# Instance normalisation over 3D volumes: the short steps run once for two tiles

## The chip, the cores and the metric

The kernel runs on one core of one Trainium2 chip. The metric is the device time of one execution in microseconds (us); smaller is better. A profiled execution of the kernel before gives the times of single instructions and of single transfers.

## The reference

```
x: (8, 64, 32, 64, 64) float32, eps = 1e-5
mean = np.mean(x, axis=(2, 3, 4), keepdims=True)
var  = np.var (x, axis=(2, 3, 4), keepdims=True)
out  = (x - mean) / np.sqrt(var + eps)
```

There are 8 x 64 = 512 instances (one for each batch and channel) of 131,072 numbers. Each instance is normalised with its own mean and variance. The input is 268.4 MB and so is the output; every number is read from memory (HBM) once and written once.

## The kernel before

**Tiles.** A tile is 8 instances, laid out as 128 partitions x 8192 floats (4 MB): an instance takes 16 partitions. There are 64 tiles. On-chip memory holds six of them, in `slot0` to `slot5`; tile k lives in slot k mod 6. The last tile is worked as two halves of 4 instances (128 x 4096), which lie side by side in slot 3.

**One tile's steps**, each done by one engine, with a semaphore from each to the next:

1. SP's queue loads the tile (L183 for the first six, L188 in the loop, L195 for the last ones).
2. VectorE (DVE) sums the left half of the columns (`reduce_sum`, L79), and ScalarE (ACT) sums the right half, by an Identity activation with an accumulator (L107). The results are two columns of a small tile.
3. TensorE multiplies the two columns by a block matrix `avg` that averages over the 16 partitions of an instance (L136, shown as two matmul passes). VectorE adds the two results and negates the sum: this is minus the mean (L82).
4. ScalarE squares the whole tile with minus the mean as its bias, and accumulates (L113). This is the longest instruction of the kernel.
5. TensorE averages the sums of squares (L143). ScalarE takes the root with eps added (L120), VectorE the reciprocal (L89) and the product with minus the mean, called the shift here (L92).
6. ScalarE normalises the left half of the columns in place (L123), VectorE the right half (L95).
7. ScalarE's queue issues the store of the tile (L130) when both are done. SP waits for this store before it loads the next tile into the same slot.

Every engine takes the tiles strictly in order, in program order: ten rounds of a loop over the six slots (60 tiles), then three single tiles and the two halves. Nothing of tile k+1 is started on ScalarE before the store of tile k is issued. On SP, the loads wait in slot order for `stored[s]`. There is one set of semaphores, one small tile and one PSUM tile for each slot (`LANES` = 8, with the two halves).

ScalarE loads a table of functions (`ACT_TABLE_LOAD`) ahead of the first L107 and the first L120 of each loop round, 20 times in all. The five engines' programs stand in an `nc.Block()`, at whose end all engines meet; ScalarE waits there for all stores first.

Of the kernel before, what the change touches and what calls it, by code (L numbers as in the profile page):

```python
# [9 lines left out]
def kernel(  # L10
# [6 lines left out]
    nc = tc.nc  # L17
    fp32 = mybir.dt.float32
    Alu = mybir.AluOpType
    Act = mybir.ActivationFunctionType  # L20

    P = 128
# [4 lines left out]

    COLS = 8192
    SLOTS = 6
    FULL = P * COLS // n_elem  # L30
    n_tiles = n_inst // FULL
    ROUNDS = (n_tiles - 1) // SLOTS
    LANES = SLOTS + 2

    x_f = x.rearrange("b c d h w -> (b c) (d h w)")
    out_f = out.rearrange("b c d h w -> (b c) (d h w)")
    x_t = x_f.rearrange("(k i) (s f) -> k (i s) f", i=FULL, s=P // FULL)
    out_t = out_f.rearrange("(k i) (s f) -> k (i s) f", i=FULL, s=P // FULL)
    x_h = x_f.rearrange("(k i) (s f) -> k (i s) f", i=FULL // 2, s=2 * P // FULL)
    out_h = out_f.rearrange("(k i) (s f) -> k (i s) f", i=FULL // 2, s=2 * P // FULL)  # L40

    ctx.enter_context(tc.tile_critical(name="norm"))  # L42

    def sbuf(name, shape, dtype=fp32):
        return ctx.enter_context(nc.sbuf_tensor(name, shape, dtype))

    slots = [sbuf(f"slot{s}", [P, COLS]) for s in range(SLOTS)]

    unused = sbuf("unused", [P, COLS], mybir.dt.uint8)
    eps_t = sbuf("eps_t", [P, 1])  # L50
    avg = {n: sbuf(f"avg{n}", [P, P]) for n in (FULL, FULL // 2)}
    small = [sbuf(f"small{i}", [P, 8]) for i in range(LANES)]
    psum = [
        ctx.enter_context(nc.psum_tensor(f"psum{i}", [P, 512], fp32))
        for i in range(LANES)
# [2 lines left out]
    def semaphores(name, n):  # L58
        return [ctx.enter_context(nc.semaphore(f"{name}{i}")) for i in range(n)]

    ready = semaphores("ready", 1)[0]
    landed = semaphores("landed", LANES)
    summed = semaphores("summed", LANES)
    meaned = semaphores("meaned", LANES)
    centred = semaphores("centred", LANES)
# [2 lines left out]
    rooted = semaphores("rooted", LANES)  # L68
    scaled = semaphores("scaled", LANES)
    shifted = semaphores("shifted", LANES)  # L70
    done = semaphores("done", LANES)
    stored = semaphores("stored", LANES)

    def on_vector(eng, t, lane, n, c1, c2, c16):
        w = t.shape[1] // 2
        a = small[lane]
        eng.reduce_sum(  # L79
            out=a[:, 0:1], in_=t[:, :w], axis=mybir.AxisListType.X  # L80
        )._wait_ge(landed[lane], c16).then_inc(summed[lane], 1)
        eng.tensor_reduce(  # L82
            out=a[:, 2:3],
            in_=psum[lane][:, 0:2],
            axis=mybir.AxisListType.X,
            op=Alu.add,
            negate=True,
        )._wait_ge(meaned[lane], c1).then_inc(centred[lane], 1)
        eng.reciprocal(out=a[:, 5:6], in_=a[:, 4:5])._wait_ge(  # L89
            rooted[lane], c1  # L90
        ).then_inc(scaled[lane], 1)
        eng.tensor_mul(out=a[:, 6:7], in0=a[:, 2:3], in1=a[:, 5:6])._wait_ge(  # L92
            scaled[lane], c1
        ).then_inc(shifted[lane], 1)
        eng.tensor_scalar(  # L95
            out=t[:, w:],
            in0=t[:, w:],
            scalar1=a[:, 5:6],
            scalar2=a[:, 6:7],
            op0=Alu.mult,  # L100
            op1=Alu.add,
        )._wait_ge(shifted[lane], c1).then_inc(done[lane], 1)

    def on_scalar(eng, t, lane, n, c1, c2, c16, dst):
        w = t.shape[1] // 2
        a = small[lane]
        eng.activation(  # L107
            out=unused[:, w : 2 * w],
            in_=t[:, w:],
            func=Act.Identity,  # L110
            accum_out=a[:, 1:2],
        )._wait_ge(landed[lane], c16).then_inc(summed[lane], 1)
        eng.activation(  # L113
            out=unused[:, : 2 * w],
            in_=t,
            func=Act.Square,
            bias=a[:, 2:3],
            accum_out=a[:, 3:4],
        )._wait_ge(centred[lane], c1).then_inc(squared[lane], 1)
        eng.activation(  # L120
            out=a[:, 4:5], in_=psum[lane][:, 2:3], func=Act.Sqrt, bias=eps_t[:, 0:1]
        )._wait_ge(varied[lane], c1).then_inc(rooted[lane], 1)
        eng.activation(  # L123
            out=t[:, :w],
            in_=t[:, :w],
            func=Act.Identity,
            scale=a[:, 5:6],
            bias=a[:, 6:7],
        )._wait_ge(shifted[lane], c1).then_inc(done[lane], 1)
        eng.dma_start(out=dst, in_=t)._wait_ge(done[lane], c2).then_inc(  # L130
            stored[lane], 16
        )

    def on_tensor(eng, t, lane, n, c1, c2, c16):
        a = small[lane]
        eng.matmul(  # L136
            out=psum[lane][:, 0:2],
            lhsT=avg[n][:],
            rhs=a[:, 0:2],
            start=True,  # L140
            stop=True,
        )._wait_ge(summed[lane], c2).then_inc(meaned[lane], 1)
        eng.matmul(  # L143
            out=psum[lane][:, 2:3],
            lhsT=avg[n][:],
            rhs=a[:, 3:4],
            start=True,
            stop=True,
        )._wait_ge(squared[lane], c1).then_inc(varied[lane], 1)


    rest = [
        (x_t[k], out_t[k], slots[k % SLOTS][:], k % SLOTS, k // SLOTS + 1, FULL)
        for k in range(ROUNDS * SLOTS, n_tiles - 1)
    ]
    last = (n_tiles - 1) % SLOTS
    for h in range(2):
        k = 2 * (n_tiles - 1) + h
        half = slots[last][:, h * COLS // 2 : (h + 1) * COLS // 2]
        rest.append((x_h[k], out_h[k], half, SLOTS + h, 1, FULL // 2))  # L160

    def over_tiles(eng, step, with_target=False):
        counts = [
            ctx.enter_context(eng.register(f"{step.__name__}_c{m}")) for m in (1, 2, 16)
        ]
        for c, m in zip(counts, (1, 2, 16)):
            eng.reg_mov(c, m)
        with eng.Fori(0, ROUNDS) as it:
            for s in range(SLOTS):
                more = (out_t[it * SLOTS + s],) if with_target else ()  # L170
                step(eng, slots[s][:], s, FULL, *counts, *more)
            for c, m in zip(counts, (1, 2, 16)):
                eng.reg_add(c, c, m)
        for _, dst, t, lane, c, n in rest:
            more = (dst,) if with_target else ()
            step(eng, t, lane, n, c, 2 * c, 16 * c, *more)

    block = ctx.enter_context(nc.Block())

    @block.sync  # L180
    def _(eng):
        for s in range(SLOTS):
            eng.dma_start(out=slots[s][:], in_=x_t[s]).then_inc(landed[s], 16)  # L183
        c16 = ctx.enter_context(eng.register("load_c16"))
        eng.reg_mov(c16, 16)
        with eng.Fori(1, ROUNDS) as it:
            for s in range(SLOTS):
                eng.dma_start(out=slots[s][:], in_=x_t[it * SLOTS + s])._wait_ge(  # L188
                    stored[s], c16
                ).then_inc(landed[s], 16)  # L190
            eng.reg_add(c16, c16, 16)
        for src, _, t, lane, c, n in rest:
            behind = lane if lane < SLOTS else last
            uses = c - 1 if lane < SLOTS else ROUNDS
            eng.dma_start(out=t, in_=src)._wait_ge(stored[behind], 16 * uses).then_inc(  # L195
                landed[lane], 16
            )

    @block.gpsimd
    def _(eng):  # L200
        count = 0
        for n, m in avg.items():
            split = P // n

            eng.memset(m[:], 1.0 / n_elem).then_inc(ready, 1)  # L205
            count += 1
            for sign in (-1, 1):
                eng.affine_select(  # L208
                    out=m[:],
                    in_=m[:],  # L210
                    pattern=[[sign * split, n], [0, split]],
                    compare_op=Alu.is_ge,
                    fill=0.0,
                    base=0 if sign < 0 else split - 1,
                    channel_multiplier=-sign,
                )._wait_ge(ready, count).then_inc(ready, 1)
                count += 1
        eng.memset(eps_t[:], eps_f).then_inc(ready, 1)  # L218

    READY = 3 * len(avg) + 1  # L220

    @block.vector
    def _(eng):
        over_tiles(eng, on_vector)

    @block.tensor
    def _(eng):
        eng.wait_ge(ready, READY)
        over_tiles(eng, on_tensor)

    @block.scalar
    def _(eng):
        eng.wait_ge(ready, READY)
        over_tiles(eng, on_scalar, with_target=True)

        for s in range(SLOTS):
            uses = ROUNDS + sum(1 for r in rest if r[3] == s)
            eng.wait_ge(stored[s], 16 * uses)
        for s in range(SLOTS, LANES):
            eng.wait_ge(stored[s], 16)  # L240


# [33 lines left out]
```

## Time and profile before

| | |
|---|---|
| four timed runs | 1248.35 to 1248.66 us, median 1248.54 us |
| the profiled execution | 1248.72 us, of which the profile's span is 1247.0 us |
| moved by the DMA queues | 536.90 MB, half in, half out |
| ScalarE (ACT) busy | 986.0 us, 79% of the span |
| VectorE (DVE) busy | 467.9 us, 38% |
| TensorE (PE) busy | 76.3 us, 6% |
| first load issued, first store issued | 1.03 us, 31.87 us |
| last store issued | 1234.04 us |

All times inside the profile are counted from the start of the span. "ACTq" and "SPq" are the instruction queues of ScalarE and SyncE, which issue stores and loads. Of the DMA queues, q1 carries the loads and q10 the stores; both are served by the same 16 DMA engines. A DMA share of 1.00 in a stretch means that these 16 were busy all the time; in short stretches the share and the rate also move a little with the transfers that lie across the edges.

### The profile page before, as it was taken

Reading aid. Unit: us, or ns where it says so; the run is one execution under the profiler, and the core shown is the slowest. Engines: PE = TensorE matmul, PEld = TensorE weight load, DVE = VectorE, ACT = ScalarE, POOL = GpSimd, SP = SyncE. Lnnn points to the kernel's source line nnn. Section 1 sums busy time; section 2 is a strip of 40 time slices with the busy share of each in tenths; the row PEclk is TensorE's granted clock in tenths of the full one; section 3 lists DMA queues with packets and bytes.
Section 4 is the critical chain, followed back from the end, with each engine's and each line's share of the span. In section 5 each row is a group of like instructions: output and inputs, shape, how many; then the busy total and the mean of one; then the engine's idle time right before and its main releaser. Section 6 shows DMA issues by size and latency. Waiting matters only on the chain.

```text
span 1247.0 us, 1819 instructions
## 1 busy us (share of the span) xinstructions
PE 76.3 (6%) x260; PEld 65.2 (5%) x260; DVE 467.9 (38%) x325; ACT 986.0 (79%) x410; POOL 1.9 (0%) x11
## 2 busy tenths in 40 slices
PE   0000000000000000000000000000000000000000
PEld 0000000000000000000000000000000000000000
DVE  2344334433334334343343433433334333343331
ACT  5888888887787878778777878787787878778774
POOL 0000000000000000000000000000000000000000
DMA  9999999999999999999999999999999999999998
GB/s 403 420 436 434 426 437 435 434 427 436 434 435 429 434 435 435 431 430 436 435 432 429 436 435 433 428 437 435 434 427 436 435 434 429 434 435 435 430 431 373
DMA packets 18722, 536.90 MB, mean 431 GB/s; under 512 B 2080, under 2 KB 2080, under 8 KB 2080
## 3 DMA queue, kind: packets, MB, share of 16 engines
q1 hardware_dynamic: 9360, 268.44, 50.0%
q10 hardware_dynamic: 9360, 268.44, 49.9%
q14 instruction: 2, 0.02, 0.0%
HBM read 268.44 MB, written 268.44 MB: 431 GB/s over the span
## 4 chain that ended last, share of the span: by engine, by line
ACT 48%; DVE 29%; another core or an unknown queue 13%; PE 6%; issue 1%; DMA 1%; ACTq 0%; DVEq 0%; SPq 0%
ACT unused L113 37%; DVE small L79 18%; DVE slot L95 8%; ACT slot L123 4%; ACT unused L107 4%; PE psum L136 3%; PE psum L143 3%; ACT small L120 1%; ACT L120 1%; DMA slot<-in_x_dram 1%; DVE small L89 1%; DVE small L82 1%; DVE small L92 1%; ACTq L130 0%
## 5 line engine op out<-in xcount | busy, mean ns | idle before, releaser
L113 ACT ACTIVATE unused<-slot,small 128x8192 uint8<-128x8192 f32 (+1 forms) x65 | 456.1, 7016 | 90.2 <-DVE small L82 90.2
L79 DVE TENSOR_REDUCE small<-slot 128x1 f32<-128x4096 f32 (+1 forms) x65 | 282.9, 4353 | 163.7 <-DMA slot<-in_x_dram 163.7
L107 ACT ACTIVATE unused<-slot 128x4096 uint8<-128x4096 f32 (+1 forms) x65 | 231.7, 3564 | 82.2 <-DMA slot<-in_x_dram 77.1
L123 ACT ACTIVATE slot<-slot,small 128x4096 f32<-128x4096 f32 (+1 forms) x65 | 243.6, 3748 | 27.6 <-DVE small L92 27.6
L89 DVE RECIPROCAL small<-small 128x1 f32<-128x1 f32 x65 | 10.7, 164 | 533.8 <-ACT small L120 533.8
L95 DVE TENSOR_SCALAR slot<-slot,small 128x4096 f32<-128x4096 f32 (+1 forms) x65 | 154.6, 2379 | 2.4
L136 PE MATMUL psum<-small,avg 128*128 128x2 f32 x130 | 38.2, 363 | 674.3 <-DVE small L79 548.8
L136 PEld LDWEIGHTS psum<-small,avg 128*128 128x128 f32 x130 | 32.6, 311 | 679.7 <-DVE small L79 553.1
L143 PE MATMUL psum<-small,avg 128*128 128x1 f32 x130 | 38.2, 363 | 480.6 <-ACT unused L113 480.6
L143 PEld LDWEIGHTS psum<-small,avg 128*128 128x128 f32 x130 | 32.6, 312 | 486.2 <-ACT unused L113 486.2
L120 ACT ACTIVATE small<-psum,eps_t 128x1 f32<-128x1 f32 x65 | 17.0, 261 | 37.4 <-PE psum L143 37.3
L82 DVE TENSOR_REDUCE small<-psum 128x1 f32<-128x2 f32 x65 | 10.3, 159 | 63.2 <-PE psum L136 63.2
L107 ACT ACT_TABLE_LOAD x10 | 12.8, 1283 | 10.4 <-ACT slot L123 7.1
L120 ACT ACT_TABLE_LOAD x10 | 12.8, 1283 | 0.2
L113 ACT ACTIVATION_READ_ACCUMULATOR unused<-slot,small 128x1 f32 x65 | 12.1, 186 | 0.0
L107 ACT ACTIVATION_READ_ACCUMULATOR unused<-slot 128x1 f32 x65 | 12.1, 186 | 0.0
L92 DVE TENSOR_TENSOR small<-small 128x1 f32<-128x1 f32 x65 | 10.3, 159 | 2.2
L208 POOL TENSOR_SCALAR_AFFINE_SELECT avg<-avg 128x128 f32<-128x128 f32 x4 | 1.3, 324 | 0.3
L205 POOL MEMSET avg<- 128x128 f32 x2 | 0.4, 204 | 0.5 <-SPq L42 0.5
L257 POOL MEMSET const-bfloat16-1.0<- 128x1 bf16 x1 | 0.1, 101 | 0.0
L257 POOL MEMSET const-uint8-127<- 128x1 uint8 x1 | 0.1, 101 | 0.0
L218 POOL MEMSET eps_t<- 128x1 f32 x1 | 0.1, 99 | 0.0
(2 smaller groups left out, 0.2 us busy)
## 6 DMA issues: line engine op xcount, KB each, us to landing
slot<-in_x_dram SPq DMA_DIRECT2D x63, 4096.0 KB, 52.6
out_dram<-slot ACTq DMA_DIRECT2D x63, 4096.0 KB, 45.4
slot<-in_x_dram SPq DMA_DIRECT2D x2, 2048.0 KB, 55.6
out_dram<-slot ACTq DMA_DIRECT2D x2, 2048.0 KB, 14.7
```

What stands on the lines that cost most here:

```text
L79: eng.reduce_sum(out=a[:, 0:1], in_=t[:, :w], axis=mybir.AxisListType.X)._wait_ge(landed[lane], c16).then_inc(summed[lane], 1)
L82: eng.tensor_reduce(out=a[:, 2:3], in_=psum[lane][:, 0:2], axis=mybir.AxisListType.X, op=Alu.add, negate=True,)._wait_ge(meaned[lane], c1) ...
L89: eng.reciprocal(out=a[:, 5:6], in_=a[:, 4:5])._wait_ge(rooted[lane], c1).then_inc(scaled[lane], 1)
L92: eng.tensor_mul(out=a[:, 6:7], in0=a[:, 2:3], in1=a[:, 5:6])._wait_ge(scaled[lane], c1).then_inc(shifted[lane], 1)
L95: eng.tensor_scalar(out=t[:, w:], in0=t[:, w:], scalar1=a[:, 5:6], scalar2=a[:, 6:7], op0=Alu.mult, op1=Alu.add,)._wait_ge(shifted[lane], ...
L107: eng.activation(out=unused[:, w : 2 * w], in_=t[:, w:], func=Act.Identity, accum_out=a[:, 1:2],)._wait_ge(landed[lane], c16).then_inc(sum ...
L113: eng.activation(out=unused[:, : 2 * w], in_=t, func=Act.Square, bias=a[:, 2:3], accum_out=a[:, 3:4],)._wait_ge(centred[lane], c1).then_in ...
L120: eng.activation(out=a[:, 4:5], in_=psum[lane][:, 2:3], func=Act.Sqrt, bias=eps_t[:, 0:1])._wait_ge(varied[lane], c1).then_inc(rooted[lane ...
L123: eng.activation(out=t[:, :w], in_=t[:, :w], func=Act.Identity, scale=a[:, 5:6], bias=a[:, 6:7],)._wait_ge(shifted[lane], c1).then_inc(don ...
L136: eng.matmul(out=psum[lane][:, 0:2], lhsT=avg[n][:], rhs=a[:, 0:2], start=True, stop=True,)._wait_ge(summed[lane], c2).then_inc(meaned[lan ...
L143: eng.matmul(out=psum[lane][:, 2:3], lhsT=avg[n][:], rhs=a[:, 3:4], start=True, stop=True,)._wait_ge(squared[lane], c1).then_inc(varied[la ...
L208: eng.affine_select(out=m[:], in_=m[:], pattern=[[sign * split, n], [0, split]], compare_op=Alu.is_ge, fill=0.0, base=0 if sign < 0 else s ...
```

## The change

Six slots are worked as three pairs. In the loop, both tiles of a pair go through each step together: the two sums, one averaging matmul over four columns, one negated addition, two squares, one averaging matmul over two columns, one root, one reciprocal, one product, then normalise and store the first tile, normalise and store the second. The rest (three single tiles, two halves) is worked one by one as before, with semaphores and small tiles of their own. `landed`, `stored` and `done` stay one for each tile; the other semaphores are one for each pair. The second square of a pair waits for the first. The table with the root is loaded once, at the start, by `preload_act_table`. The `nc.Block()` is gone: each engine's program is written straight into its queue, and SP, not ScalarE, waits for the stores at the end.

The core of the diff (`on_tensor` and the loop are changed in the same manner):

```
-    def on_vector(eng, t, lane, n, c1, c2, c16):
+    def on_vector(eng, tiles, marks, lane, n, c):
+        k = len(tiles)
...
+        for j, (t, m) in enumerate(zip(tiles, marks)):
+            eng.reduce_sum(
+                out=a[:, 2 * j : 2 * j + 1], in_=t[:, :w], axis=mybir.AxisListType.X
+            )._wait_ge(landed[m], c[16]).then_inc(summed[lane], 1)
         eng.tensor_reduce(
-            out=a[:, 2:3],
-            in_=psum[lane][:, 0:2],
+            out=a[:, 4 : 4 + k],
+            in_=psum[lane][:, 0 : 2 * k].rearrange("p (k h) -> p k h", h=2),
...
-        eng.reciprocal(out=a[:, 5:6], in_=a[:, 4:5])._wait_ge(
-            rooted[lane], c1
+        eng.reciprocal(out=a[:, 10 : 10 + k], in_=a[:, 8 : 8 + k])._wait_ge(
+            rooted[lane], c[1]
         ).then_inc(scaled[lane], 1)
...
+        for j, (t, m) in enumerate(zip(tiles, marks)):
+            eng.tensor_scalar(
+                out=t[:, w:],
...
+            )._wait_ge(shifted[lane], c[1]).then_inc(done[m], 1)
+    def on_scalar(eng, tiles, marks, lane, n, c, targets):
...
+        for j, (t, m) in enumerate(zip(tiles, marks)):
+            eng.activation(
+                out=unused[:, j * w : (j + 1) * w],
+                in_=t[:, w:],
+                func=Act.Identity,
+                accum_out=a[:, 2 * j + 1 : 2 * j + 2],
+            )._wait_ge(landed[m], c[16]).then_inc(summed[lane], 1)
+        for j, t in enumerate(tiles):
+            eng.activation(
+                out=unused[:, : 2 * w],
+                in_=t,
+                func=Act.Square,
+                bias=a[:, 4 + j : 5 + j],
+                accum_out=a[:, 6 + j : 7 + j],
+            )._wait_ge(*((squared[lane], c["odd"]) if j else (centred[lane], c[1]))).then_inc(
+                squared[lane], 1
+            )
         eng.activation(
+            out=a[:, 8 : 8 + k],
+            in_=psum[lane][:, 4 : 4 + k],
+            func=Act.Sqrt,
+            bias=eps_t[:, 0:1],
+        )._wait_ge(varied[lane], c[1]).then_inc(rooted[lane], 1)
+        for j, (t, m) in enumerate(zip(tiles, marks)):
+            eng.activation(
+                out=t[:, :w],
+                in_=t[:, :w],
+                func=Act.Identity,
+                scale=a[:, 10 + j : 11 + j],
+                bias=a[:, 12 + j : 13 + j],
+            )._wait_ge(shifted[lane], c[1]).then_inc(done[m], 1)
+            eng.dma_start(out=targets[j], in_=t)._wait_ge(done[m], c[2]).then_inc(
+                stored[m], 16
+            )
...
         with eng.Fori(0, ROUNDS) as it:
-            for s in range(SLOTS):
-                more = (out_t[it * SLOTS + s],) if with_target else ()
-                step(eng, slots[s][:], s, FULL, *counts, *more)
...
+            for g in range(GROUPS):
+                of = [g * SHARED + j for j in range(SHARED)]
+                more = ([out_t[it * SLOTS + s] for s in of],) if with_target else ()
+                step(eng, [slots[s][:] for s in of], of, g, FULL, c, *more)
...
-    block = ctx.enter_context(nc.Block())
...
+    nc.scalar.preload_act_table(Act.Sqrt)
+    nc.scalar.wait_ge(ready, set_by)
+    over_tiles(nc.scalar, on_scalar, with_target=True)
```

The order of the loads on SP, their sizes and the semaphores that they wait for are the same as before.

## The prediction

> **What bounds the kernel now.** I read the page first: the busy shares, the forty slices and the DMA queues.
>
> ```profile
> span 1247.0 us, 1819 instructions
> ...
> PE 76.3 (6%) x260; PEld 65.2 (5%) x260; DVE 467.9 (38%) x325; ACT 986.0 (79%) x410; POOL 1.9 (0%) x11
> ...
> ACT  5888888887787878778777878787787878778774
> ...
> DMA  9999999999999999999999999999999999999998
> GB/s 403 420 436 434 426 437 435 434 427 436 434 435 429 434 435 435 431 430 436 435 432 429 436 435 433 428 437 435 434 427 436 435 434 429 434 435 435 430 431 373
> ...
> q1 hardware_dynamic: 9360, 268.44, 50.0%
> q10 hardware_dynamic: 9360, 268.44, 49.9%
> ```
>
> ScalarE is the busiest engine, but no slice of it is full. The DMA row is full in every slice but the last, and the two queues together took 99.9% of the 16 engines' time. The chain of waits names ScalarE's square (37%), but a chain only follows one path back. So I asked for the stretches, to see what the DMA engines do from stage to stage:
>
> ```profile
> 5.00:30.00 25.00, 1.18 (x4) 1.00 (x4) 6.86 (x5) 14.43 (x7) 0.00 (x0) 1.00 1.02 439
> 34.00:38.00 4.00, 0.59 (x2) 0.50 (x2) 0.94 (x2) 3.13 (x3) 0.00 (x0) 1.00 1.04 385
> 200.00:1200.00 1000.00, 61.07 (x208) 52.17 (x208) 380.21 (x260) 795.59 (x329) 0.00 (x0) 1.00 1.00 433
> 1224.00:1243.00 19.00, 1.18 (x4) 1.00 (x4) 3.70 (x5) 7.75 (x6) 0.00 (x0) 1.00 0.97 417
> ```
>
> The last two columns are the DMA share and the rate. Loads alone (the first row), loads with stores (the third) and stores alone (the last) run at nearly the same rate, with a share of about 1. So the bound is the time of the 16 engines: 4.194 MB / 433 GB/s = 9.69 us for a tile one way, 128 x 9.69 = 1240 us in all. What is left of the span is 2.0 us before the first byte and about 4 us from 1243 on, in which the last engines and the closing barriers finish.
>
> The waits say the same: ScalarE waits for loads, and SP for stores, which are the DMA engines again.
>
> ```profile
> ACT unused L107 <- DMA slot<-in_x_dram: 77.1, 44, 8.9
> ...
> SPq L188 <- DMA out_dram<-slot: 1049.3, 54, 52.4
> ```
>
> **The change, part by part.** The time can only move if the DMA engines stand idle where they did not, or at the two ends.
>
> *The short steps.* The groups by line:
>
> ```profile
> L107 ACT ACT_TABLE_LOAD x10 | 12.8, 1283 | 10.4 <-ACT slot L123 7.1
> L120 ACT ACT_TABLE_LOAD x10 | 12.8, 1283 | 0.2
> ...
> L92 DVE TENSOR_TENSOR small<-small 128x1 f32<-128x1 f32 x65 | 10.3, 159 | 2.2
> ```
>
> L82, L89, L92 and L120 run 35 times instead of 65 (30 pairs and five singles). That is 30 x (159 + 164 + 159 + 261) ns = 22 us of DVE and ACT time. Of the 20 table loads one is left: 19 x 1.283 = 24.4 us of ACT. All of it is hidden by the DMA engines: 0 us. It would be worth up to 46 us if ScalarE set the pace, which it does not while it has 77 us of waiting for loads.
>
> The Trainium skill (ScalarE: Activation LUTs, "What ACT_TABLE_LOAD costs") puts a switch at about 1283 ns and 1380 ns more for a drain; the row agrees on the first, and the 0.2 us of idle time ahead of L120's loads shows no drain here. By that page the 19 would be an estimated 50 us, equally hidden.
>
> *The pair's chain.* This part could hurt: no store of a pair is issued before both tiles are squared. These rows fix the start:
>
> ```profile
> 13.53 3.62 ACT L107 ACTIVATE unused<-slot 128x4096 uint8<-128x4096 f32 x1 [8.94 <-DMA slot<-in_x_dram]
> ...
> 18.83 7.12 ACT L113 ACTIVATE unused<-slot,small 128x8192 uint8<-128x8192 f32 x1 [1.59 <-DVE small L82]
> ...
> 31.87 0.40 ACTq L130 DMA_DIRECT2D out_dram<-slot  x1
> ...
> 49.30 0.34 ACTq L130 DMA_DIRECT2D out_dram<-slot  x1
> ```
>
> Tile 0 lands at 13.5, tile 1 one tile later at 23.2. From landing to square takes 18.83 - 13.53 = 5.3, so the squares start at 28.5. Two squares with their accumulator reads take 2 x 7.31 + 0.06 = 14.7 (to 43.2); matmul, root, reciprocal and shift about 1.35 (0.68 of them between square and root, 0.68 to L123, as in the second tile); each normalise 3.80 and each store issue about 0.4. Store 0 is issued at 48.4 instead of 31.87, store 1 at 52.6. In steady work a pair costs ScalarE 2 x 3.85 + 0.86 + 14.7 + 1.35 + 2 x 4.2 = 33.0 us. The DMA engines need 2 x 19.4 = 38.8 for it. Before, the spacing of stores at full ScalarE pace is 49.30 - 31.87 = 17.4, against 19.4. So ScalarE's load falls from 90% to 85%, and it is late only at the start.
>
> *Is there always something to transfer at the start?* Before, the first store's bytes began some 4.2 us after its issue (the disturbance at 34 to 38 us), and its slot's load was issued 24.8 us after it (31.87 to 56.69). Now store 0 joins at 48.4 + 4.2 = 52.6. By then loads alone have moved about (52.6 - 2.8) / 9.69 = 5.1 of six tiles, so 8.4 us of work are left. The two queues share the engines evenly, so the loads run dry after 16.7 us, at 69.3. Store 0 is complete at about 72, the next load is issued then and joins at 73 to 76. Meanwhile store 1 runs alone; at 76 it has about half its work left and ends near 85. Store 2 is issued at 52.6 + 0.4 + 7.7 + 0.86 + 14.7 + 1.35 + 3.8 = 81.4 and joins at 85.6; load 6 then has about 5 us of work left. So about 5 us of queued transfers is the thinnest point, and no gap opens. Afterwards each pair gains 38.8 - 33.0 = 5.8 us and the queues fill. Cost: 0 us; if the chain were x us longer than 5 us, x.
>
> *A queue that starts anew.* At 34 to 38 us the stores' queue starts beside the running loads, and the rate is 385 instead of 433 GB/s: (433 - 385) / 433 x 4 = 0.44 us lost. That happens today as well. New is that the loads' queue runs dry once, at 69 to 76 us. No row shows such a restart; bounds are 0 and, with a second one near 85 us, 2 x 0.44 = 0.9. I take one, 0.44 us.
>
> The Trainium skill (DMA: Bandwidth & Descriptors, "Anatomy of one DMA — SWDGE (gpsimd) path") speaks against letting queues run dry: it gives each transfer about 2.0 us of fixed cost, for GpSimd's path. A restart at that price would make an estimated 1.6 us more than mine; no run here shows it on these queues.
>
> *The block.* Dropping it takes one meeting of all engines from the end. ScalarE's last wait for a store (L240) passes at 1245.5; the block's barrier rows lie at 1245.6 to 1245.9, and other barriers follow until 1247.0. I take -0.4 us; bounds are 0 and -1.5 (all after 1245.5).
>
> *The tail* is one by one as before. The last half landed at 1223.59 and its store was issued at 1234.04, while stores ran without a break until 1243. Pairing holds stores back, so at the end loads are further ahead and more stores are left to cover this chain: 0 us.
>
> Sum, against the profiled execution: 1248.72 + 0.44 - 0.4 = 1248.8; the median of the runs lies 0.2 below the profiled one: 1248.5 us.
>
> **Rivals.** *A: slower, the loads' queue runs dry at every tile.* A load is issued when a store has landed. If the next one always joins just after the last has ended, the queue restarts 58 times instead of once: 58 x 0.44 = 25 us, 1274 us. For: at the first turn it does run dry. Against: by my schedule load 7 is issued at about 86 while load 6 runs until about 96, and load 8 at about 105 while load 7 runs until 115; some 10 us of lead against 4.2 us to join. It decides where the lead falls below 4.2 us. A start that is several us thinner than I count (a gap of up to 5 us) lies between it and my forecast.
>
> *B: ScalarE sets the pace before and the savings show.* Then up to 46 us come off: about 1202. Against: a DMA share of 1.00 over 1000 us, at one rate in every mix. For: only the chain.
> The Trainium skill (DMA: Bandwidth & Descriptors, "Where 436 GB/s comes from") names 435 GB/s as the engines' ceiling and about 358 as the memory's share of a core; the 433 measured refutes the second here and sits at the first, so a faster rate is not to be had.
>
> *C: the change does not do what it says,* because a table load returns with every root in the loop. Then 30 or more loads of 1.283 us come back, 1.3 to 2.6 us a pair, within the 5.8 us of room: still 1248.5 in steady work, up to 1 us more at the start. It ends with the forecast.
>
> **How the numbers follow.** About 0.2% (2.5 us) is what a measurement of this kernel can tell from no change. My forecast (with C) gets 0.82, rival A and a gap at the start 0.14, B and anything else that gains over 2.5 us 0.04. The forecast's bounds give 1248.5 - 1.5 to 1248.5 + 0.9; I stretch the upper end to 1252 for part of a gap at the start, and leave out A's 1274 and B's 1202. Range 1247.0 to 1252.0.
>
> **What would show it.** Right: DMA share 1.00 and 433 GB/s over 200 to 1200 us; first stores at 48 and 52 us; one ACT_TABLE_LOAD; ScalarE busy about 986 - 24.4 - 30 x 0.26 = 954 us, and more waiting for loads than 77 us; loads resuming near 72 us; the last store issued before 1234 us. Wrong: a rate below 430 GB/s in the middle, a share below 1 at 70 to 110 us, or a span that ends more than 2.5 us from 1247.

## The result, and the profile after

| | before | after |
|---|---|---|
| median of the runs beside each other | 1248.52 us (62 runs) | 1249.87 us (42 runs) |
| ratio | | 1.002, 95% interval 1.0012 to 1.0028 |
| the profiled execution | 1248.72 us, span 1247.0 | 1248.59 us, span 1246.4 |

The change makes the kernel slower by 0.2%, a little more than its measurement is uncertain; the forecast had been "the same", 1248.5 us. Two of the 42 runs (1270.5 and 1271.8 us) are over 1.5% above the fastest, count as slow and are left out of the ratio. Over all the runs of the changed kernel, 71 with the profiled ones and the repeats told below, there are three groups: 6 cheap runs at 1248.6 to 1249.0 us (the profiled one is among them), 51 common ones at 1249.2 to 1250.5, and 14 long ones at 1252.9 to 1271.8. Of 168 runs of the kernel before one is above 1252 us (1253.3). So there are two questions: what costs the common run 1.3 us, and what makes one run in five long. Both are in the ratio.

The page of the changed kernel, in the rows that were shown of the kernel before:

```profile
span 1246.4 us, 1451 instructions
...
PE 41.1 (3%) x140; PEld 35.1 (3%) x140; DVE 448.6 (36%) x235; ACT 953.4 (76%) x361; POOL 1.9 (0%) x11
...
DMA  9999999999999999999999999999999999999998
GB/s 404 420 426 434 437 435 426 434 437 435 426 434 437 434 427 434 437 434 427 434 437 434 427 434 436 435 427 434 436 435 427 433 437 435 427 433 437 429 433 385
```

ScalarE's 986.0 us became 953.4, as worked out (954), and the DMA row did not notice. The stretches of the same execution:

```profile
34.00:38.00 4.00, 0.00 (x0) 0.00 (x0) 0.00 (x0) 3.97 (x3) 0.00 (x0) 1.00 1.04 451
200.00:1200.00 1000.00, 32.33 (x110) 27.56 (x110) 359.27 (x184) 774.36 (x288) 0.00 (x0) 1.00 1.00 433
1224.00:1243.00 19.00, 0.00 (x0) 0.00 (x0) 0.55 (x1) 1.29 (x1) 0.00 (x0) 1.00 0.98 421
```

433 GB/s and a share of 1.00 over 1000 us, exactly as before. The groups and the waits of ScalarE:

```profile
L252 ACT ACT_TABLE_LOAD x1 | 1.3, 1283 | 1.0 <-SPq L44 1.0
```

```profile
ACT unused L134 <- DMA slot<-in_x_dram: 149.8, 27, 10.9
```

One table load is left, and what ScalarE saved it spends waiting for loads: 149.8 us instead of 77.1. The order of time at the start:

```profile
28.20 7.12 ACT L141 ACTIVATE unused<-slot,small 128x8192 uint8<-128x8192 f32 x1 [1.58 <-DVE small L106]
...
35.45 7.12 ACT L141 ACTIVATE unused<-slot,small 128x8192 uint8<-128x8192 f32 x1
...
47.86 0.40 ACTq L164 DMA_DIRECT2D out_dram<-slot  x1
52.13 0.35 ACTq L164 DMA_DIRECT2D out_dram<-slot  x1
...
72.43 16.28 SPq L212 DMA_DIRECT2D slot<-in_x_dram  x2
...
80.36 0.34 ACTq L164 DMA_DIRECT2D out_dram<-slot  x1
```

Stores at 47.9, 52.1 and 80.4 us (forecast 48.4, 52.6, 81.4), the first load into a used slot at 72.4 (forecast 72). So the schedule was right to about a microsecond. But this is one of the six cheap executions: it contains neither the 1.3 us nor a long run.

### The profile page after: what moved, and what is told of

Its sections match the earlier page's. It is cut to its first block, busy times and chain, and to the rows that moved or that the text cites. A ratio compares the mean times of both kernels' runs of the same rounds, so it can differ in the third digit from the quotient of the medians.

```text
span 1246.4 us, 1451 instructions
## 1 busy us (share of the span) xinstructions
PE 41.1 (3%) x140; PEld 35.1 (3%) x140; DVE 448.6 (36%) x235; ACT 953.4 (76%) x361; POOL 1.9 (0%) x11
## 4 chain that ended last, share of the span: by engine, by line
DMA 54%; ACT 25%; another core or an unknown queue 12%; DVE 4%; PE 2%; issue 1%; ACTq 0%; SPq 0%
DMA out_dram<-slot 33%; DMA slot<-in_x_dram 21%; ACT unused L141 16%; ACT slot L157 6%; DVE small L103 4%; ACT unused L134 2%; PE psum L171 1%; PE psum L178 1%; ACT small L150 0%; ACTq L164 0%; SPq L212 0%; DVE small L113 0%; DVE small L106 0%; DVE small L116 0%
## 5 line engine op out<-in xcount | busy, mean ns | idle before, releaser
L134 ACT ACTIVATE unused<-slot 128x4096 uint8<-128x4096 f32 (+1 forms) x65 | 231.6, 3563 | 169.2 <-DMA slot<-in_x_dram 149.8
L113 DVE RECIPROCAL small<-small 128x2 f32<-128x2 f32 (+1 forms) x35 | 5.8, 165 | 498.2 <-ACT small L150 498.2
L120 DVE TENSOR_SCALAR slot<-slot,small 128x4096 f32<-128x4096 f32 (+1 forms) x65 | 152.0, 2376 | 1.3
L171 PE MATMUL psum<-small,avg 128*128 128x4 f32 (+1 forms) x70 | 20.6, 365 | 708.3 <-DVE small L103 614.9
L171 PEld LDWEIGHTS psum<-small,avg 128*128 128x128 f32 x70 | 17.6, 312 | 711.2 <-DVE small L103 617.2
L178 PE MATMUL psum<-small,avg 128*128 128x2 f32 (+1 forms) x70 | 20.5, 363 | 473.1 <-ACT unused L141 473.1
L178 PEld LDWEIGHTS psum<-small,avg 128*128 128x128 f32 x70 | 17.5, 311 | 476.1 <-ACT unused L141 476.1
L150 ACT ACTIVATE small<-psum,eps_t 128x2 f32<-128x2 f32 (+1 forms) x35 | 9.2, 262 | 23.7 <-PE psum L178 23.7
L106 DVE TENSOR_REDUCE small<-psum 128x2 f32<-128x4 f32 (+1 forms) x35 | 5.7, 162 | 40.1 <-PE psum L171 40.1
L116 DVE TENSOR_TENSOR small<-small 128x2 f32<-128x2 f32 (+1 forms) x35 | 5.6, 160 | 1.2
```

Of the source, the lines that this page charges most:

```text
L106: eng.tensor_reduce(out=a[:, 4 : 4 + k], in_=psum[lane][:, 0 : 2 * k].rearrange("p (k h) -> p k h", h=2), axis=mybir.AxisListType.X, op=Al ...
L113: eng.reciprocal(out=a[:, 10 : 10 + k], in_=a[:, 8 : 8 + k])._wait_ge(rooted[lane], c[1]).then_inc(scaled[lane], 1)
L116: eng.tensor_mul(out=a[:, 12 : 12 + k], in0=a[:, 4 : 4 + k], in1=a[:, 10 : 10 + k])._wait_ge(scaled[lane], c[1]).then_inc(shifted[lane], 1)
L120: eng.tensor_scalar(out=t[:, w:], in0=t[:, w:], scalar1=a[:, 10 + j : 11 + j], scalar2=a[:, 12 + j : 13 + j], op0=Alu.mult, op1=Alu.add,). ...
L134: eng.activation(out=unused[:, j * w : (j + 1) * w], in_=t[:, w:], func=Act.Identity, accum_out=a[:, 2 * j + 1 : 2 * j + 2],)._wait_ge(lan ...
L150: eng.activation(out=a[:, 8 : 8 + k], in_=psum[lane][:, 4 : 4 + k], func=Act.Sqrt, bias=eps_t[:, 0:1],)._wait_ge(varied[lane], c[1]).then_ ...
```

## The experiments

Edits are against the changed kernel, unless said otherwise. "60 to 95 us" is the stretch in which the loads' queue runs dry for 4 to 5 us and restarts (near 75 us), and then the stores' queue does for about 1 us (near 86 us).

### The changed kernel again, and again

No edit; the first series, the last series, and the first of four single runs:

> The changed kernel once more, for the spread of its times and for a second profile. Theory T1 (thin lead): pairing leaves the loads' queue only a few us of work when the next load joins (load latency 26.6 us in the first profile against a spacing of 19.4 us); in some executions the lead is lost, the queue runs dry at every tile, and each restart costs up to 0.44 us, so the times have a long tail from 1250 up to about 1249 + 58 x 0.4 = 1272 us. Theory T2 (the ends): the typical shift of +1.3 us (1249.87 against 1248.52) has nothing to do with the queues, but with the block's removal (time outside the span 2.1 us instead of 1.7, and the rest at the end). Both expect a median near 1249.9 and some executions above 1252 here.

> The changed kernel once more, to catch one of its long runs (above 1252 us) in the trace. Typical: median 1249.8 us, 2 of 11 above 1252. If the profile shows a long run: by theory D (the DMA engines fall out of step, a load counts as landed only when the slowest of the 16 is done) the last half lands later than in the profile at 1248.6 us and the last store is issued after 1234 us, with the rate at 432 or 433 GB/s until about 1200 us; by theory G (gaps at the start, queues dry) the rate from 60 to 95 us falls below 410 GB/s and the end keeps its shape.

> The changed kernel, one look. A common run: about 1249.8 us, or 1248.6 with a cheap restart. A long run (above 1252 us) by theory D: 433 GB/s to about 1190 us, the last half landing and the last store issued several us late, the last slice well below 371 GB/s. By theory G: below 410 GB/s from 60 to 95 us, the end as before.

The first series gave 1249.81 us (11 runs, 1248.6 to 1254.2) and its profile was once more a cheap run: 1248.60 us, 433 GB/s from 60 to 95 us. The last series gave 1249.91 us (12 runs, 1249.45 to 1270.3), and its profile is a common run at last, 1250.25 us. Its stretches:

```profile
60.00:95.00 35.00, 1.77 (x6) 1.51 (x6) 14.04 (x8) 31.30 (x12) 0.00 (x0) 1.00 1.00 418
200.00:1200.00 1000.00, 31.76 (x108) 27.07 (x108) 359.32 (x184) 774.29 (x286) 0.00 (x0) 1.00 1.00 433
```

and the same 35 us in the kernel before, with ScalarE's column alone:

```profile
60.00:95.00 35.00, 30.22 (x13) 1.00 1.00 433
```

The share is 1.00 in both, so the 16 engines do not stand idle, and yet the rate is 418 instead of 433: (433 - 418) / 433 x 35 = 1.2 us are lost by transfers that take longer. The four single runs, under one expectation, gave 1250.00, 1250.50, 1249.87 and 1250.28 us, with 416, 418, 419 and 419 GB/s in this stretch. So five common runs of the changed kernel have 416 to 419 there, and the two cheap ones 434 and 433. That is the 1.3 us between cheap and common runs. None of these profiles is of a long run.

### The block put back

```
-    load_all(nc.sync)
...
-    nc.scalar.preload_act_table(Act.Sqrt)
+    block = ctx.enter_context(nc.Block())
...
+    @block.scalar
+    def _(eng):
+        eng.preload_act_table(Act.Sqrt)
```

> Pairs and the early table load as in the changed kernel, but inside an nc.Block as before. T2: the typical time falls back to about 1248.5 plus 0.4 = 1248.5 to 1249, time outside the span 1.7 us; the tail may stay. T1: the typical time stays at 1249.5 to 1250.3 (the block's barrier adds 0.4) and the long tail stays, because the order of transfers is the same.

1249.85 us (11 runs, one long at 1265.7): the same as without the block, so the missing block is not the cause. The profile is a common run (1250.03 us), and finer stretches show both restarts (the columns as above, with ScalarE's alone):

```profile
74.00:78.00 4.00, 2.89 (x4) 1.00 0.94 360
78.00:84.00 6.00, 5.58 (x2) 1.00 0.98 421
84.00:89.00 5.00, 4.58 (x4) 1.00 1.00 354
```

The cheap profile of the changed kernel, in the same stretches:

```profile
74.00:78.00 4.00, 2.90 (x4) 1.00 1.16 500
78.00:84.00 6.00, 5.58 (x2) 1.00 1.00 431
84.00:89.00 5.00, 4.58 (x4) 1.00 1.00 433
```

The rates of 4 us stretches move with the edges (500 follows a low value), but 354 against 433 at 84 to 89 us does not. In the trace's records of single packets a full packet takes 1213 ns nearly everywhere. At 75 to 78 us, where the loads' queue restarts, 13 store packets and 7 load packets take 0.1 to 0.6 us longer; at 85 to 87 us, where the stores' queue does, 23 load packets take 0.2 to 1.0 us longer. Shared out over the 16 engines, the first restart costs 0.4 us and the second 0.9, 1.3 us together, and in the cheap profile nothing. In the five common profiles of the changed kernel the first costs 0.1 to 0.4 us and the second 0.8 to 0.9. They differ in one thing more: from load 8 to load 30 the 16 parts of a load, each with a record of its landing, land within 0.8 us of each other in the cheap profiles, and 1.6 to 3.2 us apart in the common ones. Whether that is the cause of the price or its effect, the runs don't show; and that the restarts themselves lengthen the packets is inferred from the instants.

### The first pair worked one by one

```
+    HEAD = [[0], [1], [2, 3], [4, 5]]
...
+        for i, of in enumerate(HEAD):
...
+            step(eng, [slots[s][:] for s in of], of, lane, FULL, once, *more)
...
-        with eng.Fori(0, ROUNDS) as it:
+        with eng.Fori(1, ROUNDS) as it:
```

> The changed kernel, but tiles 0 and 1 are worked one by one in an unrolled first round, with steps and semaphores of their own; tiles 2 to 59 stay pairs. The first store is issued at about 32 us instead of 48, while the loads' queue still holds three tiles, so the loads keep a lead: a latency of 38 us or more instead of 26.6, and the queue never runs dry. T1: the long tail is gone (all executions within 1 us of the median), and the median falls to 1248.2 to 1249.0. T2: the median stays at 1249.9, since the ends are those of the changed kernel; the tail may stay.

1248.58 us (12 runs: ten at 1248.1 to 1248.9, two long ones at 1255.3 and 1261.9; ratio 1.0012, 0.9993 to 1.0031). The first store is back at 31.06 us and the 1.3 us are gone (0.4 of them outside the span, see below), although 58 of the 60 tiles of the loop are still paired. The long runs are not gone.

### No pairs, but a late first store

Against the kernel before:

```
+        for i in (LANES - 2, LANES - 1):
+            eng.reduce_sum(
+                out=small[i][:, 7:8], in_=slots[0][:, :7600], axis=mybir.AxisListType.X
+            )._wait_ge(landed[0], 16)
```

> The kernel before, tiles one by one, with two more VectorE sums (128x7600 each, 16.4 us in all) ahead of the loop: the first store is issued at about 48 us as in the pairs, so the loads' queue runs dry once near 70 us and both queues start anew, with no pairing at all. T1: the first profile or the runs show the same disturbance between 60 and 95 us, 1248.5 to 1250.3 us; later stores come 17.4 us apart, so the engines may also stand idle a little at the start (up to 5 us: at most 1254). Rival (pairing itself costs, for instance by its second square's wait): 1248.5 as before.

1249.72 us (11 runs, one at 1255.4; ratio 1.0014, 1.0005 to 1.0023), with the first store at 47.52 us. So tiles worked singly with a late first store cost as much as the pairs, and pairs with an early one cost nothing. Apart from the long runs, what the pairing does in the steady part is free; its price is the instant of the first stores. The profile here is at the lower end (1249.20 us, 434 GB/s from 60 to 95 us), so it doesn't show where this kernel loses its time.

### The first stores 4 us and 1 us later

```
+    nc.scalar.activation(
+        out=idle[:], in_=slots[0][:, :960], func=Act.Identity, accum_out=idle_sum[:]
+    )._wait_ge(landed[1], 16)
```

> The changed kernel with one more ScalarE instruction ahead of the loop, a 128x960 Identity on slot 0 into a tile of its own that waits for tile 1 (about 1.0 us), which makes the first pair's chain 1 us later. T1: the lead of the loads' queue gets thinner by about as much, so more executions fall into the slow range: median 1252 to 1272, load latency near 24 us. T2: every execution as in the changed kernel, +0 to +1 us.

This delayed the stores by 4 us, not 1 (51.91 and 56.18 us), and it took **1248.57 us** (11 runs, 1248.3 to 1249.2), 1.3 us less than the changed kernel, where 1252 or more was expected. The rate from 60 to 95 us is 434 GB/s. So the queue of transfers is not thin enough for a delay to open a gap, and the restarts at this instant cost nothing. The shorter delay:

```
+    nc.vector.reduce_sum(
+        out=small[LANES - 1][:, 15:16],
+        in_=slots[0][:, :6000],
+        axis=mybir.AxisListType.X,
+    )._wait_ge(landed[0], 16)
```

> The changed kernel with one more VectorE sum (128x6000 of slot 0, about 6.5 us) ahead of the loop, which makes the second tile's sum, and with it the first pair's stores, 1.3 us later. The late kernel of the first set moved them by 4 us and lost the usual +1.3 us. T1: where the restarts at 75 and 86 us fall against the running packets decides their price, so a shift of 1.3 us may give anything between 1248.5 and 1250.3; the profile's rate over 60 to 95 us tells which: 433 GB/s in a cheap run, 417 in a dear one. A thin start (a true gap of the engines) would show as a time that grows with the delay: 1251 here.

1249.45 us (11 runs, none long), stores at 48.83 and 53.10 us, 416 GB/s from 60 to 95 us. So 1 us later the restarts are dear and 4 us later they are free. Which of the two it is isn't a matter of how late; the runs give no rule for it.

### Three tiles at a time

```
-    SHARED = 2
+    SHARED = 3
```

> The changed kernel with SHARED = 3: two groups of three tiles instead of three pairs (the small tiles get wider columns, the scratch tile of the sums is half as wide again, the rest of the tiles is as before). Three tiles are held back at a time, so fewer transfers are queued and both queues run dry again and again: by the schedule worked out from the rows the loads' queue some 56 times, the stores' some 20 times, while all 16 engines stand idle together only at the start, for about 5 us. Theory T1 (a restarted queue costs 0.3 to 0.5 us beside the running one): 1248.5 + 5 + 56 x 0.3..0.5 = 1270 to 1282 us, with stretches below 433 GB/s all along the middle. Rival T0 (a restart costs nothing as long as the other queue has work): 1253 to 1256 us, and 433 GB/s in the middle.

1260.05 us (6 runs, 1254.4 to 1268.8; ratio 1.0107, 1.0079 to 1.0136). The profile is the lowest run, 1254.36 us:

```profile
60.00:95.00 35.00, 31.76 (x13) 1.00 0.86 351
200.00:1200.00 1000.00, 770.34 (x280) 1.00 1.00 433
```

```profile
slot<-in_x_dram SPq DMA_DIRECT2D x63, 4096.0 KB, 23.3
```

Here a real gap opens: the first store is issued at 65.11 us, when all six tiles have been loaded (2.8 + 6 x 9.69 = 61 us), and the share falls to 0.86, 0.14 x 35 = 4.9 us of idle engines; with the longer packets of the two restarts behind it, the rate of 351 GB/s makes (433 - 351) / 433 x 35 = 6.6 us lost. This is what a start that is too thin looks like, and the pairs show nothing of the kind. The last row is the median from a load's issue to its landing: 23.3 us, of which some 19.4 are the transfer itself at half rate, so a load hardly ever finds another one ahead of it. By the records of the packets, the loads' queue has nothing in transfer for over 2.2 us 10 times after 100 us, and the stores' queue 16 times (neither ever does in the kernel before), and the middle still has 433 GB/s: after 100 us, longer packets cost only some 0.5 us more in all than in the kernel before. So in this run the later restarts cost next to nothing, and the two at the start are the exception. What the other runs, up to 14 us longer, are made of, no profile here shows.

### The long runs: the kernel before without its block

Against the kernel before: no block, SP waits for the stores at the end, and the table of functions loaded early.

```
-    block = ctx.enter_context(nc.Block())
...
+    load_all(nc.sync)
+    wait_all(nc.sync)
+    set_up(nc.gpsimd)
+    over_tiles(nc.vector, on_vector)
...
+    nc.scalar.preload_act_table(Act.Sqrt)
+    nc.scalar.wait_ge(ready, READY)
+    over_tiles(nc.scalar, on_scalar, with_target=True)
```

> The kernel before with only the last part of the change: no nc.Block, SP waits for the stores at the end, one early table load; tiles one by one. T2 (the ends cost the 1.3 us): 1249.3 to 1249.9. T1 (the queues' restarts do): 1248.1 to 1248.7, no long tail, every load some 52 us from issue to landing.

**1257.87 us** (5 runs, 1256.7 to 1259.9; ratio 1.0076, 1.0063 to 1.0089), where both theories had 1248 to 1250. Two further kernels took this apart. The first only drops the block (the same edit without the early table):

```
-    nc.scalar.preload_act_table(Act.Sqrt)
```

> The kernel before without its block, and nothing else: the table of functions is loaded in the first tile's chain as before, so the first store is issued near 31.9 us. The single version without a block and with an early table took 1257.9 us, with the last half landing about 12 us later than before. Theory S (the first store's instant decides: 0.8 us earlier put the 16 DMA engines out of step from the start): 1248 to 1249.5 us here, the last store issued near 1234 us. Theory B (what the missing block changes, SP waiting at the end and the engines' entry, costs): 1256 to 1260 us, the last store near 1246 us. For the pairs, S means that the tail of long runs is a matter of the engines' step, and that the missing block cost nothing; B means that the missing block is dear where tiles are worked singly.

1248.34 us (11 runs; ratio 0.9999, 0.9990 to 1.0007). The second keeps the block and only loads the table early:

```
+        eng.preload_act_table(Act.Sqrt)
         eng.wait_ge(ready, READY)
         over_tiles(eng, on_scalar, with_target=True)
```

> The kernel before with its block, and only the table of functions loaded early: one table load, first store near 31.1 us instead of 31.9. The mirror of the run above. Theory S: 1255 to 1260 us, the last store issued near 1246 us. Theory B: 1247.5 to 1249 us, the last store near 1234 us. If both of these runs stay near 1248.5, only the two edits together cost the 9 us; if both are near 1257, either does.

**1259.21 us** (7 runs: six at 1258.2 to 1285.7, one at 1248.7). Taking 19 table loads out of an engine that has time to spare costs 10.6 us (1248.64 beside it). What it changes for the transfers is that the first store is issued at 31.14 us instead of 31.87. The order of time at its end: ScalarE's sum of the last half, which starts when that half has landed, and the last store:

```profile
1235.36 1.91 ACT L107 ACTIVATE unused<-slot 128x2048 uint8<-128x2048 f32 x1 [0.86 <-DMA slot<-in_x_dram]
...
1245.81 0.34 ACTq L130 DMA_DIRECT2D out_dram<-slot  x1
```

the same two rows without the block, in a run of 1248.39 us:

```profile
1223.48 1.91 ACT L107 ACTIVATE unused<-slot 128x2048 uint8<-128x2048 f32 x1 [0.94 <-DMA slot<-in_x_dram]
...
1233.93 0.34 ACTq L130 DMA_DIRECT2D out_dram<-slot  x1
```

and the rate of the long one, with its wait for loads:

```profile
GB/s 400 417 433 434 434 434 433 434 434 433 434 434 433 434 434 433 434 433 434 434 430 434 434 434 433 434 434 433 433 434 433 434 434 432 432 434 430 434 417 254
```

```profile
ACT unused L107 <- DMA slot<-in_x_dram: 111.2, 55, 11.2
```

The middle runs at the full rate, and by bytes the loads are as far ahead of the stores as before (3.25 tiles at 600 us; 3.29 in the kernel before). Yet the last half counts as landed 12 us later, a load takes 56.2 us from issue to landing (52.6 before), and ScalarE waits for 55 loads instead of 44. The reason is in the records of single landings. A load has 16 of them, and it has landed with the last:

| spread of the 16 landings of a load, us | tile 5 | tile 20 | tile 40 | the last half |
|---|---|---|---|---|
| the kernel before | 0.9 | 1.3 | 2.1 | 2.8 |
| early table, 1259.21 us | 2.1 | 5.4 | 8.9 | 13.9 |
| no block and early table, 1259.14 us | 2.2 | 6.1 | 9.5 | 14.1 |

With the early table, 15 of the 16 parts of the last half have landed at 1223.3 us, as in the kernel before (1223.1 for all 16), and the sixteenth lands at 1235.0. Without the block as well, it is three parts that come at 1233.8 to 1235.2. The packets agree: after 100 us, 117 full packets take over 20 ns longer than 1213 ns, 12.4 us together, with one part late; 272 do, 32.2 us together, with three parts late; and 6 do, 0.2 us together, in the kernel before. So one or a few of the 16 fall behind all through the run, by some 11 to 12 us each, which an average over 16 hardly shows; this is theory D of the expectations above. Then ScalarE's chain of 10.5 us to the last store, covered by remaining stores before, stands open: the last slice falls from 373 to 254 GB/s.

The lag is there at tile 5, which lands near 90 us. After the one in the first tile's chain, the next table load of the kernel before comes at 119.58 us, so up to there the two kernels differ only in that everything behind the first tile's root is 0.7 us earlier on ScalarE. But the instant of the first store alone doesn't decide it: one of seven runs of this very kernel took 1248.68 us, and the first pair worked apart, with its first store at 31.06 us, has a spread of 2.6 us at tile 5 and only 3.1 at the end. What makes the lag grow is open.

### The pairs' first stores a little earlier and a little later

Two runs asked whether the instant of the first store brings the pairs' long runs as well: 7/16 of each sum to VectorE and 9/16 to ScalarE, and the extra sum of above with 2500 columns.

```
-                out=a[:, 2 * j : 2 * j + 1], in_=t[:, :w], axis=mybir.AxisListType.X
+                out=a[:, 2 * j : 2 * j + 1], in_=t[:, : w * 7 // 8], axis=mybir.AxisListType.X
...
-                in_=t[:, w:],
...
+                in_=t[:, w * 7 // 8 :],
```

> VectorE sums 7/16 of each tile and ScalarE 9/16 (8 to 8 before), in every pair: the wait of the first square shrinks, and the first store is issued about 0.4 us earlier, near 47.4 us. ScalarE gets 0.9 us more work a pair, within its room. If the instant of the first store brings the long runs (theory S): their share changes from about 1 in 5, most likely up, with the last half landing late in a long profile. If they are a matter of the pairing whatever the instant: 1 to 4 of 11 above 1252 us, as before. The common run in both: 1249.5 to 1250.3 us.

```
+        in_=slots[0][:, :2500],
```

> One extra VectorE sum over 2500 columns of the first tile; the first store is issued about 0.3 us later, near 48.2 us, between the changed kernel and the run with 6000 columns (48.83 us, no long run in 11). Theory S: fewer long runs than 1 in 5, or none. Pairing whatever the instant: 1 to 4 of 11 above 1252 us. The common run in both: 1249.4 to 1250.0 us.

The first moved the store only to 47.78 us, 0.1 earlier: 1249.98 us, 1 of 12 above 1252 (1252.5). Its profile, 1251.58 us, is the longest of a kernel with pairs here, and has 410 GB/s from 60 to 95 us: (433 - 410) / 433 x 35 = 1.9 us lost in that stretch, so the price of the restarts can go above 1.2 us too. The second moved it to 48.17: 1249.59 us, 1 of 12 above 1252 (1275.5). With the delays of 1 and 4 us that makes 1 long run of 34 with a later store, against 14 of 71 of the changed kernel. This speaks for the instant, but 0.1 us earlier did not bring more, as the theory wanted, and no profile shows a long run of the pairs. It stays open.

## Why the prediction was wrong

The mechanism and the schedule were right, two terms of the sum were mis-sized, and one outcome was missing.

- **The bound**, the savings hidden, the pair's chain, "no gap opens": right, as the rows above show. The share at 70 to 110 us never fell, and the last store was issued at 1225 to 1228 us, earlier than 1234. Rival B is refuted by 433 GB/s with 33 us less work on ScalarE, rival C by the single table load. Rival A, a restart at every tile, is refuted for the pairs by 433 GB/s in the middle of all their profiles.
- **"A queue that starts anew" is the step that failed.** It took one restart at 0.44 us, with 0.9 for two as the upper bound. Two restarts came (75 and 86 us), and together they cost 1.2 us in common runs and 0 in cheap ones. In the common runs the loads' restart, which the sum had at 0.44, costs 0.1 to 0.4; the stores' restart, which stood only in the upper bound, costs 0.8 to 0.9. The price had been read from the one start that the trace of before has, at 34 to 38 us, as if it were the same each time; it is not. (That start costs 0.6 us by the records of its packets; the 0.44 from a stretch of 4 us moves with the edges.)
- **The block** was taken at -0.4 us. For tiles worked singly it is -0.3 (1248.34 against 1248.64 beside it); for the pairs it is 0 (1249.81 without, 1249.85 with). With the block gone 2.1 us lie outside the pairs' span, instead of 1.8 to 1.9 with it and 1.7 in the kernel before, and that eats what the end of the span gains. The missing block alone does not make it: the first pair apart and the two extra VectorE sums have no block either, and 1.7 to 1.8 us. Why is open.
- **The sum** thus misses 1.2 - 0.44 = 0.8 and 0.4: 1248.5 + 1.2 = 1249.7, against 1249.87 measured.
- **The long runs** appear in no step. With a range of 1247 to 1252 for the median that did not show, but they are about half of the 0.2% in the ratio (2.5 us, of which 1.35 is the difference of the medians). The prediction named no case in which one of the 16 parts of the transfers falls behind the others. The single version with the early table shows that such a case exists, and what it costs, 10 us at the end. That the pairs' long runs are the same is not shown.
- The rule of the Trainium skill that was weighed (DMA: Bandwidth & Descriptors, "Anatomy of one DMA — SWDGE (gpsimd) path", about 2.0 us of fixed cost for a transfer, on GpSimd's path) would have put two restarts near 4 us as an estimate. The pairs' runs show 0 to 1.9 us for the two on these queues, and the triples' middle at 433 GB/s shows many restarts for next to nothing.

The edits that were to save time saved none, because the 16 DMA engines set the pace. One experiment, the stores 4 us later, brings the changed kernel back to 1248.57 us, level with the kernel before. Nothing here beats it beyond what can be measured.

## What to carry to other kernels

Where the DMA engines are the bound, an edit on another engine is worth what it does to the instants at which loads and stores are issued. So write down the first stores and the first re-used slot, and give the restart of a queue that runs dry a range from nothing to well above the one restart that the trace happens to show. A share of 1.00 is not yet the full rate: read the GB/s beside it in the stretch that has changed. An average over 16 engines also hides one that falls behind: compare the landings of one transfer's parts, above all of the last load. And take the profile of more than one execution before you explain a difference of 0.1%, since the one at hand may be of the cheap kind.

## What the runs showed that was not expected

- A queue that restarts beside a running one stretches some 20 packets (1.2 us each) by 0.1 to 1.0 us, in some runs, and none in others of the same kernel.
- With the first store 0.7 us earlier (31.14 instead of 31.87 us), a kernel that is bound by transfers took 1259 instead of 1248.5 us in six of seven runs, at the same rate of 433 GB/s through the middle: in the profiled run one of the 16 parts of the transfers fell behind the others by 12 us, little by little, and the last load was late by as much.
